# A decoder trunk in three-pass matmuls: the down projection as seven block products, interleaved with the next up projection

## Chip, cores, metric

The kernel runs on one core of a Trainium2 chip. The metric is the device time of one execution in microseconds (us); lower is better. In the profile PE is TensorE's matmuls and PEld its weight loads, DVE is VectorE, ACT is ScalarE, POOL is GpSimd, and SP is SyncE, which issues the loads of the weights.

## What is computed

Two pre-norm residual layers over 256 tokens with 2048 features. Each has a mixer (different kinds of attention, with one input and one output projection) and an MLP of hidden size 8192. The change touches the MLPs alone:

```python
D_MODEL = 2048; SEQ = 256; DEPTH = 2; D_FF = 4 * D_MODEL

def squared_relu_mlp(h, w_up, w_down):
    return jnp.square(jax.nn.relu(h @ w_up)) @ w_down

for layer in range(DEPTH):
    ...                                  # x = x + mixer(rms_norm(x))
    h = rms_norm(x, mlp_norm[layer])
    x = x + squared_relu_mlp(h, w_up[layer], w_down[layer])
return rms_norm(x, final_norm)
```

Everything is float32 in and out.

## The kernel before

**Three passes.** A float32 operand is split into a high half, rounded to the float32r format, and a low half, which is what is left. A product runs as wh·xh + wh·xl + wl·xh, summed in PSUM. Activations lie with features on the partitions, and an operand tile is `[xh | xl]`, 512 columns for 256 tokens. So for one K-tile (128 rows of K) and one column tile (128 columns of the weight) the kernel issues two matmuls with a piece of the weight as the stationary operand: one of 512 columns (wh against both halves, line 445) and one of 256 (wl against xh, line 446). That is the block kind "T". Some blocks of the mixers are of kind "N": there the activations are stationary and the weights move, in three matmuls of 256 columns (lines 434 to 436). The very last block of the program, kind "last", has weights stationary and three matmuls of 256 columns (lines 440 to 442).

**The weight stream.** All weights go through one list, `stream`, in the order in which TensorE uses them. An element is a chunk: 4 K-tiles x 256 columns, 16 matmuls. A `Unit` is one load from DRAM by SP (1 MB, 4 K-tiles x 512 columns, rows of 2 KB) and feeds two chunks. `hi_to` makes a chunk's high half with an ACT copy (line 1077), `lo_to` its low half with a DVE subtraction (line 1085), and `consume` issues the matmuls. There are 3 buffers for raw loads, 5 for high halves and 4 for low halves. The main loop for chunk i is, in this order:

```python
        hi_to(i + HI_BUFS)      # written up to the high half of chunk i + 4
        lo_to(i + LO_BUFS)      # written up to the low half of chunk i + 3
        chunk(i)                # the matmuls, and at a block's end its evacuation
        ...                     # jobs.tick(): side work (attention, norms, splits)
```

The order is fixed (a manual schedule), and each engine runs its own instructions in that order. The low half of chunk i + 3 lies in the buffer of chunk i - 1, the high half of chunk i + 4 in that of chunk i - 1 too.

**The MLP** (`mlp`). The hidden features are cut into two groups of 4096. For a group, the up projection runs in pairs of blocks of 256 columns, with 16 K-tiles each. `up_done` adds the two halves of PSUM, squares the positive part and splits the result into `h` (lines 935 to 937, 156, 157). Then the group's down projection runs as 8 blocks with 32 K-tiles each; `down_done` adds the result to the residual `xT` (lines 951 to 955). The low half of every chunk is made by DVE. POOL's queue issues hardly anything: a few constants, `odist`, `sk` and `fn`.

Of the kernel before, what the change touches and what calls it, by code (L numbers as in the profile page):

```python
# [38 lines left out]
class Jobs:  # L39
    """Side work (attention, norms, splits) that is woven between the weight chunks."""  # L40
# [48 lines left out]
class Ring:  # L89
    """Order of use of the buffers of one tag: a buffer is free once its key is done."""  # L90
# [13 lines left out]
class Unit:  # L104
    """One load: up to 4 K-tiles x 512 columns of a weight, for one or two chunks."""
# [5 lines left out]
class Chunk:  # L111
    """Some K-tiles of a block: views(raw) are the parts of the load in the order of the operand."""

    def __init__(self, unit, kts, views):
        self.unit, self.kts, self.views = unit, kts, views
        unit.users += 1


class Block:
    """256 output columns of one projection (128 where tiles is 1)."""  # L120

    def __init__(self, kind, chunks, mov, done, tiles=2):
        self.kind, self.chunks, self.mov, self.done, self.tiles = kind, chunks, mov, done, tiles
        self.total = sum(len(c.kts) for c in chunks)
        self.count, self.ps = 0, None
# [3 lines left out]
def trunk(ctx, tc, x, attn_norm, mlp_norm, w_up, w_down, ev_w_in, ev_q_norm, ev_w_uq, ev_kv_norm,  # L129
# [5 lines left out]
    psum = ctx.enter_context(tc.tile_pool(name="psum", bufs=1, space=bass.MemoryType.PSUM))  # L135
    ctx.enter_context(tc.manual_schedule())
# [48 lines left out]
    # the tensor engine's clock rises while the first loads are under way  # L185
    def keep_warm(n):
        if "warm" not in st:
            st["warm"] = psum.tile([P, 2, 512], F32, name="mm", bufs=3)[:, 0]
        ps = st["warm"]
        for _ in range(n):  # L190
            mm(ps, warm[:, 0:P], warm, start=True, stop=True)
# [19 lines left out]
    def make_xs(b, g0):  # L211
        """Next phase's moving operand from residual block b, and its sum of squares."""
# [19 lines left out]
    def sum_squares(acc, ms, size):  # L232
        """ms [P, 2] <- mean square + eps per token, tokens on partitions."""
# [5 lines left out]
    def broadcast(r, rB):  # L239
        """rB [P, T] <- r [P, 2] along the free axis, on every partition."""  # L240
# [46 lines left out]
    def w_chunks(w, c0, groups, width=512):  # L287
        """Loads of K-tile groups x width columns of w [K, N]: the chunks of each 256 columns."""
# [23 lines left out]
    def evac(ps, dst, scale=None, rB=None):  # L312
        """dst [P, 2, T] <- sum of the bank halves, times scale, times rB along tokens."""
# [11 lines left out]
    def scores(pairs, dist, cs, u):  # L325
        """u [P, 2, 384] <- biased logits of two heads: [q0 k0 | q1 k0 | q1 k1]."""
# [9 lines left out]
    def neg_max(u, nm):  # L336
        """nm [P, 2 (q tile), 2 (head)] <- -max."""
# [13 lines left out]
    def transpose_p(u):  # L351
        """In place: [k0 q0 | k0 q1 | k1 q1]."""
# [55 lines left out]
    stream = []  # L408

# [4 lines left out]
    def consume(block, i, hi, lo):  # L414
        if block.ps is None:
            block.ps = psum.tile([P, 2, 512], F32, name="mm", bufs=3)
            if block.kind == "last":
                block.ps = [block.ps[:, 0, 0:T], psum.tile([P, 2, 512], F32, name="mm", bufs=3)[:, 0, 0:T]]
# [9 lines left out]
        for n, j in order:  # L428
# [10 lines left out]
            if block.kind == "last":  # L439
# [14 lines left out]
    def even_mixer():  # L454
# [5 lines left out]
        def open_pool():  # L460
            pool = E["pool"] = pool_ctx.enter_context(tc.tile_pool(name="even", bufs=1, reuse_waits="tile"))
# [78 lines left out]
        # the shared rotary key, on both partition halves  # L540
# [11 lines left out]
        def rotate(src, n, outs):  # L552
            """outs <- src*cos + swap(src)*sin; src [P, n, T]."""
# [29 lines left out]
        # per-head projections  # L583
# [38 lines left out]
        def cut(view, pr, width, a, b):  # L622
            """The columns a:b of the two heads, width columns each, of a load."""
# [68 lines left out]
        # output projection  # L692
# [18 lines left out]
    def odd_mixer():  # L711
# [7 lines left out]
        def open_pool():  # L719
            pool = E["pool"] = pool_ctx.enter_context(tc.tile_pool(name="odd", bufs=1, reuse_waits="tile"))  # L720
# [78 lines left out]
        # dilated groups: slots 2*sp, 2*sp+1 of the three groups, one joint softmax  # L799
# [112 lines left out]
    def mlp(layer, last):  # L912
# [6 lines left out]
        def open_pool():  # L919
# [316 lines left out]
```

## Time and profile before

| what | value |
|---|---|
| time, three runs | 2188.19, 2188.74, 2188.99 us (median 2188.74) |
| span of the profiled execution | 2186.0 us; no time of that execution around its span is shown, and the median of the runs is 2.7 us longer |
| PE busy | 2173.6 us, 99% |
| DVE busy | 1298.6 us, 59% |
| ACT busy | 1022.6 us, 47% |
| POOL busy | 12.8 us |
| DMA | 396 MB, 181 GB/s over the span |

A matmul's duration in the profile is from its start to the modelled end of its pipeline, and overlaps the next one. So what a matmul costs is read from the distance of the starts. DVE and ACT instructions overlap a little too when they follow one another.

### The profile page before, as it was taken

The page shows a single profiled execution, that of the slowest core. Times are in us where ns is not written, and L with a number is a line of the kernel's source. Part 1 is how long each engine was busy: PE and PEld are TensorE (multiplying, and loading weights), DVE is VectorE, ACT ScalarE, POOL GpSimd, SP SyncE. Part 2 cuts the span into 40 slices and gives each one's busy share as a digit, 9 for nine tenths or more (in the row PEclk, how much of TensorE's full clock was granted, in tenths as well). Part 3 has the DMA queues.
Part 4 walks back from the last instruction along what each step waited for, and adds up shares of the span by engine and source line. Part 5 has one row for each costly group of instructions (what it writes and reads, how often), then busy time and mean ns, then how long its engine had stood idle before and what let it go on. Part 6 is the DMA issues. An engine that isn't in the chain of part 4 may idle for free.

```text
span 2186.0 us, 31244 instructions
## 1 busy us (share of the span) xinstructions
PE 2173.6 (99%) x12902; PEld 1917.1 (88%) x12902; DVE 1298.6 (59%) x1576; ACT 1022.6 (47%) x1377; POOL 12.8 (1%) x24
## 2 busy tenths in 40 slices
PE   9999999999999999999999999999999999999998
PEld 7898988888888888888888889988888888888887
DVE  6766666656545565556667665566565556655554
ACT  6554544444434444444445446444443334444443
POOL 0000000000000000000000000000000000000000
PEclk9999999999999999999999999999999999999999
DMA  8544455555555555655654456665555555555544
GB/s 260 182 149 155 147 188 184 184 194 175 198 187 192 191 182 187 207 190 176 188 166 148 154 174 190 158 193 184 186 183 199 185 184 189 192 185 183 191 154 135
DMA packets 211374, 396.26 MB, mean 181 GB/s; under 512 B 8904, under 2 KB 31504, under 8 KB 211104
## 3 DMA queue, kind: packets, MB, share of 16 engines
q1 hardware_dynamic: 210720, 392.33, 55.3%
q8 instruction: 101, 1.65, 0.3%
q0 software_dynamic: 480, 1.94, 0.3%
q14 instruction: 41, 0.34, 0.0%
q10 hardware_dynamic: 32, 0.01, 0.0%
HBM read 392.15 MB, written 2.10 MB: 180 GB/s over the span
## 4 chain that ended last, share of the span: by engine, by line
PE 99%; DMA 0%; ACT 0%; SPq 0%; DVE 0%; POOLq 0%; issue 0%; ACTq 0%; DVEq 0%
PE mm L445 55%; PE mm L446 30%; PE mm L448 3%; PE mm L435 2%; PE mm L434 2%; PE mm L436 2%; PE side L333 1%; PE side L356 1%; PE side L402 1%; PE side L331 1%; PE mm L442 0%; PE mm L440 0%; PE mm L441 0%; PE side L403 0%; DMA latqs<-ev_w_in 0%; PE side L873 0%
## 5 line engine op out<-in xcount | busy, mean ns | idle before, releaser
L1085 DVE TENSOR_TENSOR lo<-raw,hi 128x1024 fp32r<-128x1024 f32 (+1 forms) x756 | 898.6, 1194 | 627.2 <-PE mm L446 555.4
L1077 ACT ACTIVATE hi<-raw 128x1024 fp32r<-128x1024 f32 (+1 forms) x756 | 780.6, 1036 | 804.9 <-PE mm L445 712.4
L445 PE MATMUL mm<-xs,hi 128*128 128x512 f32 x2805 | 995.3, 396 | 0.5 <-ACT hi L1077 0.3
L446 PE MATMUL mm<-xs,lo 128*128 128x256 f32 x2992 | 820.5, 279 | 0.2 <-DVE lo L1085 0.2
L445 PE MATMUL mm<-h,hi 128*128 128x512 f32 x1922 | 675.0, 393 | 0.0
L445 PEld LDWEIGHTS mm<-xs,hi 128*128 128x128 f32 x2805 | 526.0, 188 | 121.1 <-ACT hi L1077 1.0
L446 PEld LDWEIGHTS mm<-xs,lo 128*128 128x128 f32 x2992 | 561.4, 188 | 8.8 <-DVE lo L1085 0.5
L446 PE MATMUL mm<-h,lo 128*128 128x256 f32 x1984 | 548.7, 279 | 0.0
L445 PEld LDWEIGHTS mm<-h,hi 128*128 128x128 f32 x1922 | 360.2, 187 | 84.4
L446 PEld LDWEIGHTS mm<-h,lo 128*128 128x128 f32 x1984 | 371.9, 187 | 2.8
L434 PE MATMUL mm<-hi,xs 128*128 128x256 f32 x320 | 91.8, 287 | 0.0
L936 DVE TENSOR_TENSOR t<-mm,t 128x512 f32<-128x512 f32 x64 | 44.3, 691 | 77.3 <-ACT t L935 77.3
L436 PE MATMUL mm<-hi,xs 128*128 128x256 f32 x320 | 89.7, 280 | 0.0
L435 PE MATMUL mm<-lo,xs 128*128 128x256 f32 x320 | 89.7, 280 | 0.0
L935 ACT ACTIVATE t<-mm 128x512 f32<-128x512 f32 x64 | 38.3, 598 | 100.3 <-PE mm L448 100.3
L448 PE MATMUL mm<-xs,hi 128*128 128x512 f32 x187 | 69.9, 396 | 0.0
L445 PE MATMUL mm<-oT,hi 128*128 128x512 f32 x192 | 67.6, 394 | 0.0
L435 PEld LDWEIGHTS mm<-lo,xs 128*128 128x128 f32 x320 | 60.3, 188 | 0.2
L434 PEld LDWEIGHTS mm<-hi,xs 128*128 128x128 f32 x320 | 60.3, 188 | 0.2
L436 PEld LDWEIGHTS mm<-hi,xs 128*128 128x128 f32 x320 | 60.2, 188 | 0.0
L446 PE MATMUL mm<-oT,lo 128*128 128x256 f32 x192 | 53.6, 279 | 0.0
L315 ACT ACTIVATE t<-mm 128x512 f32<-128x512 f32 x37 | 22.1, 598 | 53.8 <-PE mm L448 53.8
(266 smaller groups left out, 1494.3 us busy)
## 6 DMA issues: line engine op xcount, KB each, us to landing
raw<-w_up SPq DMA_DIRECT2D x128, 1024.0 KB, 5.3
raw<-w_down SPq DMA_DIRECT2D x120, 1024.0 KB, 5.0
raw<-od_w_in SPq DMA_DIRECT2D x36, 1024.0 KB, 5.1
raw<-ev_w_in SPq DMA_DIRECT2D x30, 1024.0 KB, 5.4
raw<-ev_w_out SPq DMA_DIRECT2D x16, 1024.0 KB, 5.0
raw<-od_w_in SPq DMA_DIRECT2D x20, 512.0 KB, 4.1
raw<-od_w_out SPq DMA_DIRECT2D x16, 512.0 KB, 6.0
raw<-w_down SPq DMA_DIRECT2D x16, 512.0 KB, 3.6
```

Of the source, the lines that this page charges most:

```text
L315: act(t, ps[:, :, T:], AF.Copy, scale=1.0 if scale is None else scale)
L331: mm(ps[:, 0:P], q[:, 0:P], k[:, 0:P], start=(i == 0), stop=(i == n - 1))
L434: mm(o, xh, hi[:, n], start=first, stop=False)
L435: mm(o, xh, lo[:, n], start=False, stop=False)
L436: mm(o, xl, hi[:, n], start=False, stop=last)
L445: mm(ps[:, j], hi[:, n, c], m, start=first, stop=False)
L446: mm(ps[:, j, 0:T], lo[:, n, c], m[:, 0:T], start=False, stop=False)
L448: mm(ps[:, j], hi[:, n, c], m, start=False, stop=True)
L935: act(t, ps[:, :, T:], AF.Copy)
L936: tt(t, ps[:, :, 0:T], t, op=OP.add)
L1077: act(d, r, AF.Copy)
L1085: tt(d, r, f32(h), op=OP.subtract)
```

## The change

The hidden features are cut into eight groups of 1024. In seven of the eight, the down projection is computed in block products: for two K-tiles, two halves of the tokens and two halves of 512 output columns, the eight products of a 2 x 2 block multiplication become seven, of sums and differences of the blocks. Each is again three matmuls of 256 columns, with the activation as the stationary operand. The last group stays plain (kind "T", one block at a time).

- `up_done` makes the sums of the activation blocks (`S1` to `S4`) with four small DVE operations and splits all seven with one ACT and one DVE operation.
- A product unit is still a load of 4 K-tiles x 512 columns; it feeds four chunks: `plain` (two blocks, 12 matmuls), `single` (one block, 6 matmuls), `13` and `24` (12 each). The weight sums of the last two are made by DVE in `prep13` and `prep24` before the split.
- The seven products of a 512-column stretch gather in four PSUM banks over a group (`s0`: three of them, `s1`: four). ACT copies them to SBUF, and a DMA on POOL's queue writes them to a DRAM tile (`sums`), adding to it from the second group on. After the seventh group `combine` reads a tile back, forms the four results, scales them with the token norms, turns them with TensorE and adds them to `xT`.
- Up blocks become kind "U": three matmuls of 256 columns in place of a pair, all into 256 columns of PSUM; their load is 8 K-tiles x 256 columns (rows of 1 KB) and feeds two chunks.
- The stream of a group's products is interleaved with the next group's up projection: two product chunks, one up chunk, and so on. The first group's up projection and the last group's down projection stand alone.
- For every second up chunk from the second group on (`again`), the low half isn't made by DVE: ACT writes the negated, rounded weights into the low half's buffer, and a DMA on POOL's queue adds the weights from DRAM to it.
- Comments are taken out, and the PSUM banks are opened by phase.

```diff
-        NGRP = 2
+        NGRP = 8
         W = FF // NGRP
...
+    X11, X22, X12, S1, S2, S3, S4 = range(7)
+    HOME = {1: ("s0", 0), 2: ("s0", 1), 3: ("s0", 2), 5: ("s1", 0), 7: ("s1", 1), 6: ("s1", 2), 4: ("s1", 3)}
...
+            if block.kind == "U":
+                mm(ps[:, j], hi[:, n, c], m[:, 0:T], start=first and j == 0, stop=False)
+                mm(ps[:, j], hi[:, n, c], m[:, T:], start=False, stop=False)
+                mm(ps[:, j], lo[:, n, c], m[:, 0:T], start=False, stop=last and j == 1)
...
+    def consume_products(block, i, hi, lo):
...
+        for o, (a, prod) in enumerate(chunk.prods):
+            half, at = HOME[prod]
+            if half not in block.ps:
+                block.ps[half] = banks(half, 1)
+            ps = block.ps[half].rearrange("p b c -> p (b c)")[:, at * T:(at + 1) * T]
+            for q, pr in enumerate(chunk.kts):
+                x = block.mov(pr)
...
+                mm(ps, x[:, a, 0:P], hi[:, o, q], start=first and at % 2 == 0, stop=False)
+                mm(ps, x[:, a, 0:P], lo[:, o, q], start=False, stop=False)
+                mm(ps, x[:, a, P:], hi[:, o, q], start=False, stop=last and (at % 2 == 1 or prod == 3))
+        block.count += 1
+        if block.count == block.total - 2:
+            block.done("s0", block.ps["s0"])
+        if block.count == block.total:
+            block.done("s1", block.ps["s1"])
...
         def up_done(grp, b):
             def f(ps):
-                r = E["pool"].tile([P, 2, T], F32, name="hr", bufs=3)
                 t = temp()
-                act(t, ps[:, :, T:], AF.Copy)
-                tt(t, ps[:, :, 0:T], t, op=OP.add)
-                stt(r, t, 0.0, t, op0=OP.max, op1=OP.mult)
+                act(t, ps, AF.Relu)
+                r = E["pool"].tile([P, 8, P], F32, name="hr", bufs=1)
+                act(r[:, 0:4].rearrange("p (j k) t -> p j (k t)", j=2), t, AF.Square)
...
+                        tt(r[:, 4], r[:, 0], r[:, 2], op=OP.add)
+                        tt(r[:, 6], r[:, 1], r[:, 0], op=OP.subtract)
+                        tt(r[:, 5], r[:, 4], r[:, 1], op=OP.subtract)
+                        tt(r[:, 7], r[:, 3], r[:, 5], op=OP.subtract)
+                        act(h[:, :, 0:P], r[:, 1:8], AF.Copy)
+                        tt(h[:, :, P:], r[:, 1:8], f32(h[:, :, 0:P]), op=OP.subtract)
...
+                def prep13(unit=unit, made=made):
+                    w = blocks(unit.raw)
+                    t = made[13] = E["pool"].tile([P, 1024], F32, name="w13")
+                    tt(four(t), w[:, :, :, 1].rearrange("p q k c -> p k q c"),
+                       w[:, :, 0].rearrange("p q h c -> p h q c"), op=OP.subtract)
+
+                def prep24(unit=unit, made=made):
+                    w = blocks(unit.raw)
+                    t = made[24] = E["pool"].tile([P, 1024], F32, name="w24")
+                    tt(four(t)[:, 0], four(made[13])[:, 1], w[:, :, 0, 0], op=OP.add)
+                    tt(four(t)[:, 1], w[:, :, 1, 0], four(t)[:, 0], op=OP.subtract)
...
+                chunks += [Chunk(unit, ks, plain, prods=((X11, 1), (X12, 2))),
+                           Chunk(unit, ks, single, prods=((S4, 3),)),
+                           Chunk(unit, ks, of(13), prep13, ((S1, 5), (S3, 7))),
+                           Chunk(unit, ks, of(24), prep24, ((S2, 6), (X22, 4)))]
...
+        def products_done(grp, cb):
+            def f(half, ps):
+                n = 3 if half == "s0" else 4
+                stage = E["pool"].tile([P, 4 * T], F32, name="stage", bufs=2)[:, 0:n * T]
+                act(stage, ps.rearrange("p b c -> p (b c)")[:, 0:n * T], AF.Copy)
+                to = sums[cb][:, 0:n * T] if half == "s0" else sums[cb][:, 3 * T:]
+                if grp == 0:
+                    nc.gpsimd.dma_start(to, stage)
+                else:
+                    nc.gpsimd.dma_start(to, stage, accum_op=OP.add)
+                if grp == NGRP - 2 and half == "s1":
+                    jobs.spawn(combine(cb), keys=[("sum", cb)], delay=1)
...
+        def combine(cb):
+
+            s = E["pool"].tile([P, 7, 2 * P], F32, name="hs", bufs=2 * nb)
+            nc.gpsimd.dma_start(s, sums[cb].rearrange("p (o c) -> p o c", o=7))
+            yield 3, 0
...
+        stream.extend(up_list(0))
+        for grp in range(NGRP - 1):
+            s, u = product_list(grp), up_list(grp + 1)
+            for i in range(len(u)):
+                stream.extend(s[2 * i:2 * i + 2] + u[i:i + 1])
...
+            prep = stream[i][0].chunks[stream[i][1]].prep
+            if prep:
+                prep()
             for d, r in views(i, his[i]):
                 act(d, r, AF.Copy)
...
+            again = stream[i][0].chunks[stream[i][1]].again
             for (d, r), (h, _) in zip(views(i, los[i]), views(i, his[i])):
-                tt(d, r, f32(h), op=OP.subtract)
+                if again is None:
+                    tt(d, r, f32(h), op=OP.subtract)
+                else:
+                    act(d, r, AF.Copy, scale=-1.0)
+                    nc.gpsimd.dma_start(d.rearrange("p (k c) -> p k c", c=T), again, accum_op=OP.add)
```

## Rows read from the trace of the kernel before

**Rows 1.** The page: span, busy times by engine, and the chain by engine.
```profile
span 2186.0 us, 31244 instructions
...
PE 2173.6 (99%) x12902; PEld 1917.1 (88%) x12902; DVE 1298.6 (59%) x1576; ACT 1022.6 (47%) x1377; POOL 12.8 (1%) x24
...
PE 99%; DMA 0%; ACT 0%; SPq 0%; DVE 0%; POOLq 0%; issue 0%; ACTq 0%; DVEq 0%
```
**Rows 2.** Timeline of PE, first MLP: start, duration, engine, line, operation, tiles, count.
```profile
798.76 0.39 PE L445 MATMUL mm<-xs,hi 128*128 128x512 f32 x1
799.00 0.28 PE L446 MATMUL mm<-xs,lo 128*128 128x256 f32 x1
799.11 0.39 PE L445 MATMUL mm<-xs,hi 128*128 128x512 f32 x1
```
**Rows 3.** Timeline of PE, kind "N", second mixer: first and last of 100 starts.
```profile
1364.76 0.28 PE L436 MATMUL mm<-hi,xs 128*128 128x256 f32 x1
...
1376.37 0.28 PE L436 MATMUL mm<-hi,xs 128*128 128x256 f32 x1
```
**Rows 4.** Timeline of PE, kind "last": first and last of 28 starts.
```profile
2168.33 0.28 PE L441 MATMUL mm<-h,hi 128*128 128x256 f32 x1
...
2171.57 0.28 PE L441 MATMUL mm<-h,hi 128*128 128x256 f32 x1
```
**Rows 5.** Timeline of DVE, then of ACT, first MLP; in brackets idle time before.
```profile
639.28 1.23 DVE L1085 TENSOR_TENSOR lo<-raw,hi 128x1024 fp32r<-128x1024 f32 x1 [1.56 <-PE mm L446]
642.08 1.23 DVE L1085 TENSOR_TENSOR lo<-raw,hi 128x1024 fp32r<-128x1024 f32 x1 [1.57 <-PE mm L446]
...
639.16 1.06 ACT L1077 ACTIVATE hi<-raw 128x1024 fp32r<-128x1024 f32 x1 [1.79 <-PE mm L445]
641.96 1.06 ACT L1077 ACTIVATE hi<-raw 128x1024 fp32r<-128x1024 f32 x1 [1.74 <-PE mm L445]
```
**Rows 6.** Groups by line and form: busy us, mean ns; idle before, its releasers.
```profile
L1085 DVE TENSOR_TENSOR lo<-raw,hi 128x1024 fp32r<-128x1024 f32 x716 | 872.8, 1222 | 614.1 <-PE mm L446 551.0 <-PE mm L435 36.2 <-issue 18.8
L1077 ACT ACTIVATE hi<-raw 128x1024 fp32r<-128x1024 f32 x716 | 757.4, 1059 | 788.0 <-PE mm L445 700.4 <-issue 25.2 <-DMA raw<-w_down 17.5
...
L1085 DVE TENSOR_TENSOR lo<-raw,hi 128x512 fp32r<-128x512 f32 x40 | 25.8, 686 | 13.1 <-issue 7.1 <-PE mm L446 4.4 <-PE mm L435 1.6
L1077 ACT ACTIVATE hi<-raw 128x512 fp32r<-128x512 f32 x40 | 23.2, 624 | 16.9 <-PE mm L445 12.1 <-issue 3.1 <-DMA raw<-od_w_in 0.9
```
**Rows 7.** The chain in order of time: start, us, four transposes at the program's start.
```profile
16.04 0.44 PE side L1110 x4
```
**Rows 8.** Timeline of DVE and of ACT where nothing is waited for.
```profile
1079.07 1.22 DVE L1085 TENSOR_TENSOR lo<-raw,hi 128x1024 fp32r<-128x1024 f32 x1
1080.21 0.68 DVE L952 TENSOR_TENSOR t<-mm,t 128x512 f32<-128x512 f32 x1
...
2127.53 1.05 ACT L1077 ACTIVATE hi<-raw 128x1024 fp32r<-128x1024 f32 x1
2128.48 0.62 ACT L227 ACTIVATE t<-xT 128x512 f32<-128x512 f32 x1
```
**Rows 9.** DMA issues over the span: count, KB each, median us to landing.
```profile
raw<-od_w_in SPq DMA_DIRECT2D x20, 512.0 KB, 4.1
...
raw<-w_down SPq DMA_DIRECT2D x16, 512.0 KB, 3.6
...
fn<-final_norm POOLq DMA_DIRECT2D x1, 1024.0 KB, 5.7
odist<-c_dist POOLq DMA_DIRECT2D x1, 768.0 KB, 6.8
...
sk<-od_sinks POOLq DMA_DIRECT2D x1, 8.0 KB, 2.8
```
**Rows 10.** DMA in 1080 to 1110, 2130 to 2160, 1500 to 1600 us.
```profile
q1 hardware_dynamic: 6336, 6.29, 67.3%
...
raw<-od_w_in SPq DMA_DIRECT2D x14, 512.0 KB, 4.5
...
q1 hardware_dynamic: 5647, 5.60, 59.2%
...
raw<-w_down SPq DMA_DIRECT2D x10, 512.0 KB, 4.5
...
q1 hardware_dynamic: 9503, 18.88, 57.9%
```

More of the change, by code (lines that the diff above doesn't have):

```diff
@@ L111, with __init__ @@
 class Chunk:
-    def __init__(self, unit, kts, views):
-        self.unit, self.kts, self.views = unit, kts, views
+    def __init__(self, unit, kts, views, prep=None, prods=(), again=None):
+        self.unit, self.kts, self.views, self.prep, self.prods = unit, kts, views, prep, prods
+        self.again = again
         unit.users += 1
 class Block:
-    def __init__(self, kind, chunks, mov, done, tiles=2):
+    def __init__(self, kind, chunks, mov, done, tiles=2, take=None):
         self.kind, self.chunks, self.mov, self.done, self.tiles = kind, chunks, mov, done, tiles
-        self.total = sum(len(c.kts) for c in chunks)
+        self.total = len(chunks) if kind == "S" else sum(len(c.kts) for c in chunks)
+        self.take = take
         self.count, self.ps = 0, None
@@ L414, in consume @@
     def consume(block, i, hi, lo):
+        if block.kind == "S":
+            return consume_products(block, i, hi, lo)
         if block.ps is None:
-            block.ps = psum.tile([P, 2, 512], F32, name="mm", bufs=3)
-            if block.kind == "last":
-                block.ps = [block.ps[:, 0, 0:T], psum.tile([P, 2, 512], F32, name="mm", bufs=3)[:, 0, 0:T]]
+            block.ps = (block.take or banks)()
         ps, tiles, kts = block.ps, block.tiles, block.chunks[i].kts
@@ L451, in consume @@
             block.done(ps)
+    def consume_products(block, i, hi, lo):
+        chunk = block.chunks[i]
+        if block.ps is None:
+            block.ps = {}
+        n = len(chunk.prods)
+        hi = hi[:, 0:n * 2 * T].rearrange("p (o q c) -> p o q c", q=2, c=T)
+        lo = lo[:, 0:n * 2 * T].rearrange("p (o q c) -> p o q c", q=2, c=T)
+        for o, (a, prod) in enumerate(chunk.prods):
[5 more added lines that the diff above has]
+                x = block.mov(pr)
+                first, last = block.count < 4 and q == 0, block.count >= block.total - 4 and q == 1
+                mm(ps, x[:, a, 0:P], hi[:, o, q], start=first and at % 2 == 0, stop=False)
[6 more added lines that the diff above has]
+            block.done("s1", block.ps["s1"])
     def even_mixer():
@@ L948, in f, with finish, down_done @@
+        left = [2] * 8
+        def finish(b):
+            left[b] -= 1
+            if left[b] == 0:
+                if last:
+                    final_block(E, b)
+                else:
+                    x_done(b, g_next, 2)
+        def down_done(b):
             def f(ps):
@@ new lines, in f, with eights, load, views @@
+                finish(b)
+            return f
+        def eights(w, c0, n, by_dma=False):
+            view = w.rearrange("(k p) c -> p k c", p=P)
+            chunks = []
+            for a in range(0, n, 8):
+                def load(raw, a=a):
+                    nc.sync.dma_start(raw.rearrange("p (k c) -> p k c", c=T), view[:, a:a + 8, c0:c0 + T])
+                unit = Unit(load)
+                for h in range(2):
+                    def views(raw, dst, h=h):
+                        return [(dst, raw[:, h * 1024:(h + 1) * 1024])]
+                    k = a + 4 * h
+                    chunks.append(Chunk(unit, list(range(k, k + 4)), views,
+                                        again=view[:, k:k + 4, c0:c0 + T] if h and by_dma else None))
+            return chunks
@@ new lines, in up_list, with product_list, mov @@
+        def up_list(grp):
+            blocks = [Block("U", eights(up, grp * W + b * T, KT, grp > 0), mov, up_done(grp, b), take=take_up)
+                      for b in range(nb)]
+            return [(block, i) for block in blocks for i in range(len(block.chunks))]
+        def product_list(grp):
+            def mov(pr):
+                need(("h", layer, grp, pr))
+                return hs[grp, pr]
+            blocks = [Block("S", product_chunks(down[grp * W:(grp + 1) * W], cb * 512), mov, products_done(grp, cb))
+                      for cb in range(4)]
+            return [(block, i) for block in blocks for i in range(len(block.chunks))]
@@ new lines, in mlp, with h_mov @@
+        stream.extend(up_list(0))
[3 more added lines that the diff above has]
+                stream.extend(s[2 * i:2 * i + 2] + u[i:i + 1])
+        def h_mov(kt):
+            need(("h", layer, NGRP - 1, kt // 2))
+            return hs[NGRP - 1, kt // 2][:, kt % 2]
+        wd = down[FF - W:]
+        for b in range(8):
+            if last and b == 7:
+                add(Block("last", eights(wd, b * T, W // P), h_mov, lambda ps: last_block(E, ps), take=take_last))
+            else:
+                add(Block("T", eights(wd, b * T, W // P), h_mov, down_done(b), take=take_down(b)))
@@ L1189, in trunk @@
         block, c = stream[i]
-        if block.tiles * len(block.chunks[c].kts) == 8:
+        if block.tiles * len(block.chunks[c].kts) == 8 or block.kind == "S" and c % 2:
             jobs.tick()
```

102 lines of the change are left out of this document (73 added, 29 removed).

## The prediction

> **What bounds the kernel now.** I read the page's busy times and chain first: TensorE is busy for 99% of the 2186.0 us and carries 99% of the chain that ended last [rows 1]. So only two things can change the time: the matmul work itself, and a new wait in front of a matmul. Next I read the spacing of matmul starts, because the modelled durations overlap: a 512-column matmul and the 256-column one behind it take 0.350 us together (798.76 to 799.11) [rows 2]. Where three 256-column matmuls stand in place of such a pair, 99 starts take 11.61 us, 0.1173 us each, with activations as the stationary operand [rows 3]; with weights stationary and the tokens moving, as in the very last block, 27 starts take 3.24 us, 0.120 us each [rows 4]. None of them waits for its weight load. Last I read how far the splitters run ahead: in the MLP, ACT makes a high half and DVE a low half every 2.80 us, the time of one chunk on TensorE, and each starts when TensorE gives a buffer back [rows 5]; over the span that is what ended most of their idle time [rows 6]. So a low half is started when its buffer comes free, four chunks ahead, and no earlier. It has three chunks of TensorE time to be finished in. Today that is 8.4 us for a 1.2 us operation.
>
> **The change on TensorE.** Seven of eight groups of a down projection become products. A group was 8 K-tiles x 16 column tiles = 128 pairs, 128 x 0.350 = 44.8 us. It becomes 16 block products of 7 x 3 matmuls, 336 x 0.1173 = 39.4 us (the stationary operand is an activation, as in rows 3). Over 14 groups: -75.4 us. The up projections' 2 x 1024 pairs become three 256-column matmuls; weights are stationary, so rows 4 is nearest: 0.360 for 0.350, +20.5 us (by rows 3 it would be +3.9). Putting the sums back turns 64 blocks of 128x128; four of them take 0.44 us [rows 7], +7.0 us. The first up group and the last, plain down group have no partner and cost what they cost today. Together 2186.0 - 75.4 + 20.5 + 7.0 = 2138.1 us for the profiled span, or 2121.5 with the cheap up chunks. The median of the runs is 2.7 us above that span, so **2141** (2124) if nothing waits.
>
> **The change on DVE and ACT.** The stream repeats a period of six chunks: two product chunks (12 and 6 matmuls), an up chunk (24), two product chunks (12, 12), an up chunk (24). On TensorE: 42 x 0.1173 + 48 x 0.120 = 10.69 us; there are 8 per group, 14 groups, 112 periods. Back to back a 1024-column operation costs DVE 1.14 us and ACT 0.95 us from start to start [rows 8]; 512 columns cost up to 0.69 and 0.62 [rows 6]. DVE per period: low halves of three product chunks and one up chunk 4 x 1.14, of the short chunk 0.69, prep13 1.14, prep24 2 x 0.69, and half of the four small adds and the split in `up_done` (about 2 us, an estimate from the same rows), 1.0: 8.8 us, 82%. Without the DMAs it would be 9.9. ACT: six high halves 5 x 0.95 + 0.62, one negated copy 0.95, half of two stagings (0.7 and 0.95) and of `up_done`'s work (about 2): 8.1 us, 76%. Both fit, and their in-order queues have three chunks of cover; I cost them at nothing. If DVE missed it, a period would grow by what it lacks, and no more.
>
> **The wait that is added.** Every second up chunk no longer gets its low half from DVE. ACT writes minus the rounded weights, and a DMA on POOL's queue adds the weights from DRAM. It has the same place in the stream: its buffer comes free when the short product chunk ends, and it is needed after one up chunk and two product chunks: 2.88 + 1.41 + 1.41 = 5.70 us. In that time ACT first makes the next high half, whose buffer came free at the same moment and which is written ahead of it (0.95), then the negated copy (1.06), and in every second period the staging of the first three products stands before both (0.7, three quarters of 0.95): 2.36 us on average. What is left for the DMA from issue to landing is 3.34 us. TensorE goes through the chunks in order, so what is missing is idle time, and the loop starts again only when the chunk is done: it is paid 112 times. Queued behind the waiting DMA on POOL are the next group's stagings and, late, the read-back of the sums, none of them near their use.
>
> No such accumulating DMA is in this trace, so I bound its landing by rows. Below: 2.8 us, an 8 KB load from POOL; then it is hidden. 512 KB weight loads land in 3.6 to 4.1 us as a median over the span [rows 9], and in 4.5 us in the two stretches of 512 KB loads, at 59 and 67% of the DMA engines [rows 10]. Above: 5.7 us for 1 MB and 6.8 us for 768 KB from POOL [rows 9]. If an accumulation reads both its operands, it moves as much as 1 MB does. When it is issued the engines are not idle: the up unit's load is released at the end of the chunk before, and the next product unit's by the same negated copy. I take **4.7 us**, nearest to the 4.5 of the same bytes beside a busy stream. Then 4.7 - 3.34 = 1.36 us per period, x 112 = 152 us. By the ends: 0 and (6.8 - 3.34) x 112 = 388 us.
>
> The Trainium skill, "Collectives: The Full Stack", section "The bandwidth ceiling: the fold count and why AG ≠ RS ≠ AR", speaks against the change: an add inside a DMA reads two sources, and a transfer with it ran at 1/1.93 of the rate of a plain one. No run here shows such an add yet. By an estimate from that factor, 512 KB would land like 1 MB of [rows 9], and the sum would be 2402 instead of 2290 us.
>
> **Other costs.** The stagings write 128x768 and 128x1024 to DRAM, from POOL, accumulating from the second group on; their PSUM halves are next used some 8 us later, and ACT empties them in under 1 us, so nothing. The read-back waits for the last staging to land (about 5 us) and itself for about 5 us, while its adds come three ticks (about 8 us) later in DVE's order: up to 2 or 3 us of DVE waiting, eight times, 0 to 24 us; the low halves' lead covers that, I take 0 and keep 24 for the range. Up loads change from rows of 2 KB to 1 KB, which cost no more: 5.6 MB in 30 us at a 59.2% share and 18.88 MB in 100 us at 57.9% [rows 10] are 315 and 326 GB/s of a full share.
>
> **Rivals.**
> *A, the forecast:* TensorE waits for DMA-made low halves, 2138 + 152 = 2290, as a median **2293**.
> *B, hidden:* the DMA lands within 3.3 us and the arithmetic wins: **2141**, 2124 with cheap up chunks. For it: 2.8 us for a small POOL load, 3.6 us for 512 KB. The point at which it decides is a landing of 3.34 + (2189 - 2141)/112 = 3.77 us; below, the kernel is faster than before. Against it: every 512 KB row of a stretch of its own is above 4.
> The Trainium skill, "DMA: Bandwidth & Descriptors", section "Anatomy of one DMA — SWDGE (gpsimd) path", gives 2.0 us plus the bytes over 436 GB/s; by that estimate 512 KB take 3.2 us, nothing is missing, and the sum is B's. The traces speak rather against: 1 MB from POOL took 5.7 us beside the stream, where the fit gives 4.4.
> *C, the DMA engines become the bound:* a period moves two loads of 1.05 MB, 0.52 MB added to low halves and 0.46 MB of staging; counted twice where it accumulates, 4.06 MB. At 326 GB/s that is 12.5 us against 10.69, x 112 = +198 us, **2339**. Counted once it is 3.08 MB, 9.4 us, and no bound. The waits would then end on `raw` loads as well, not on low halves alone.
> *D, the products are not there, or the splitters bind:* if DVE ran at its full durations (1.22 for 1.14) it would need about 9.3 us of 10.69, still no bound; that gives B's time.
>
> **How the numbers follow.** A 0.50, B with D 0.33 (of it 0.03 with a landing so near 3.77 us that nothing is seen), C 0.17 (of it 0.02 near no change). A measurement of this kernel tells about 0.2% from no change. So faster 0.30, same 0.05, slower 0.65. The range takes in B's 2141 and a little of its cheap end, and A with a landing of about 6.3 us, (6.3 - 3.34) x 112 = 332 us, with some of the read-backs: 2130 to 2480. A's own range is 2190 to 2480.
>
> **What will show it.** In the changed profile TensorE's share falls to about 93%, with idle time in front of the up chunks' matmuls that read `lo`, ended by DMA `lo<-w_up`; these DMAs are 112 and land in 4 to 6 us. A product chunk of 12 matmuls takes 1.41 us and an up chunk 2.88 us. DVE stands near 80% inside the product stretch. If the DMAs land in 3.3 us and TensorE stays at 99%, B is right and my landing time wrong; if it waits for `hi` or `raw`, C is; if DVE has no idle time left, D's sum was wrong.

## The result and the profile after

The changed kernel takes 3362.7 us (median of 4 runs, 3353.4 to 3366.6) against 2188.5 us: 1.536 times the time before, 95% interval 1.534 to 1.538. It is slower, as forecast, but by 1174 us where 104 were forecast, and far outside the range of 2130 to 2480. In the experiments below a time that stands without an interval is that of a single run.

Lines of the page of the changed kernel: span and busy times, the granted clock (PEclk) and the DMA queues. They answer to [rows 1]; the second fence has the clock and the load queue of the kernel before.

```profile
span 3351.6 us, 39749 instructions
...
PE 2383.0 (71%) x16086; PEld 2275.5 (68%) x16086; DVE 1631.1 (49%) x2136; ACT 1431.5 (43%) x1889; POOL 256.5 (8%) x256
...
PE   9999956665565566665899999666655566666667
...
PEclk9999987777787777777999999777777778778778
...
q1 hardware_dynamic: 280224, 392.32, 36.9%
q0 software_dynamic: 76384, 119.39, 20.6%
```
```profile
PEclk9999999999999999999999999999999999999999
...
q1 hardware_dynamic: 210720, 392.33, 55.3%
```

TensorE is busy for 71% of the span where it was 99%, and its idle slices are the two product stretches. In the same slices the granted clock is 0.7 to 0.8; before it was full nearly throughout. DVE and ACT have more work than before (1631 and 1432 us busy), but over the longer span DVE's share fell to 49% and ACT's to 43%, and the load queue's fell from 55% to 37%; POOL's queue rose from 0.3% to 20.6%. No engine is near its limit. This is a wait, not a shortage of an engine.

The waits of the changed kernel (who waited for whom, us in total, times, longest) name it, and the DMA issues (count, KB, median us to landing; last, for the low halves, minimum, median and maximum) show what came so late; they answer to [rows 9].

```profile
PE up L467 <- DMA lo<-w_up: 945.8, 112, 11.2
...
raw<-w_up SPq DMA_DIRECT2D x128, 1024.0 KB, 7.1
raw<-w_down SPq DMA_DIRECT2D x128, 1024.0 KB, 5.9
lo<-w_up POOLq DMA_DIRECT2D x112, 512.0 KB, 9.0
...
DMA to landing us min/median/max: 7.6/9.0/12.8
```

There are 112 waits, one per period, 8.4 us each in the mean, all in front of the first matmul that reads a DMA-made low half. The accumulating DMA lands after 9.0 us in the median, 7.6 at the least and 12.8 at the most.

The timeline of two periods shows the whole loop. The first fence is PE at the two waits and around the first, the second ACT and POOL before them, the third the loads that SP starts just before POOL's DMAs.

```profile
899.16 0.28 PE L465 MATMUL up<-xs,hi 128*128 128x256 f32 x1
...
902.04 0.28 PE L498 MATMUL s<-hi,hs 128*128 128x256 f32 x1
...
904.89 0.28 PE L465 MATMUL up<-xs,hi 128*128 128x256 f32 x1
...
915.27 0.55 PE L467 MATMUL up<-xs,lo 128*128 128x256 f32 x1 [9.98 <-DMA lo<-w_up]
915.62 0.42 PE L465 MATMUL up<-xs,hi 128*128 128x256 f32 x1
915.83 0.42 PE L466 MATMUL up<-xs,hi 128*128 128x256 f32 x1
...
922.08 0.29 PE L465 MATMUL up<-xs,hi 128*128 128x256 f32 x1
...
936.37 0.55 PE L467 MATMUL up<-xs,lo 128*128 128x256 f32 x1 [8.18 <-DMA lo<-w_up]
```
```profile
899.68 0.79 ACT L1074 ACTIVATE stage<-s 128x768 f32<-128x768 f32 x1
900.37 1.05 ACT L1280 ACTIVATE hi<-raw 128x1024 fp32r<-128x1024 f32 x1
901.31 1.04 ACT L1292 ACTIVATE lo<-raw 128x1024 fp32r<-128x1024 f32 x1
...
902.65 1.30 POOL L1293 DMA_DIRECT2D lo<-w_up  x1 [1.00 <-ACT lo L1292]
...
924.66 0.95 ACT L1017 ACTIVATE hs<-hr 128x896 fp32r<-128x896 f32 x1 [1.33 <-DVE hr L1016]
925.52 1.04 ACT L1280 ACTIVATE hi<-raw 128x1024 fp32r<-128x1024 f32 x1
926.47 1.05 ACT L1292 ACTIVATE lo<-raw 128x1024 fp32r<-128x1024 f32 x1
...
927.81 1.30 POOL L1293 DMA_DIRECT2D lo<-w_up  x1 [19.94 <-ACT lo L1292]
```
```profile
902.38 0.37 SPq L1031 DMA_DIRECT2D raw<-w_down  x1
...
927.54 0.37 SPq L1031 DMA_DIRECT2D raw<-w_down  x1
```

At 899.16 the up chunk starts whose predecessor gave the buffer back. It takes 2.88 us, the two product chunks 2.85 us, and at 904.89 the waiting chunk starts: 5.73 us of lead, as worked out. But POOL issues the DMA at 902.65, 3.5 us after the buffer came free, because ACT does the staging, the next high half and the negated copy first; and it lands 12.6 us later. In the next period the buffer comes free at 922.08 and the issue is at 927.81, 5.7 us later: ACT's order there holds the splitting of the activations, which itself waits 1.33 us for DVE. That DMA lands in 8.6 us. In both periods the same negated copy lets SP start a load of 1 MB, 0.27 us ahead of POOL's DMA. The two periods alternate over the whole trace: half of the 112 DMAs have a staging DMA in flight when they are issued and land in 11.2 us in the mean, the others in 8.6. Over all 112 the mean way to the issue is 4.5 us and the mean landing 9.9; with 5.7 us of lead that leaves 8.7 us, of which the chunk's first two matmuls hide 0.2.

After each wait the matmul starts are 0.21 us apart (915.62 to 915.83) in place of 0.12: the lower of the two clock levels, 1.2 GHz.

### The profile page after: what moved, and what is told of

Its sections match the earlier page's. It is cut to its first block, busy times and chain, and to the rows that moved or that the text cites. A ratio compares the mean times of both kernels' runs of the same rounds, so it can differ in the third digit from the quotient of the medians.

```text
span 3351.6 us, 39749 instructions
## 1 busy us (share of the span) xinstructions
PE 2383.0 (71%) x16086; PEld 2275.5 (68%) x16086; DVE 1631.1 (49%) x2136; ACT 1431.5 (43%) x1889; POOL 256.5 (8%) x256
## 3 DMA queue, kind: packets, MB, share of 16 engines
q0 software_dynamic: 76384, 119.39, 20.6%
## 5 line engine op out<-in xcount | busy, mean ns | idle before, releaser
L467 PE MATMUL up<-xs,lo 128*128 128x256 f32 x2048 | 694.5, 339 | 945.8 <-DMA lo<-w_up 945.8
L467 PEld LDWEIGHTS up<-xs,lo 128*128 128x128 f32 x2048 | 493.2, 241 | 965.0 <-issue 965.0
L465 PE MATMUL up<-xs,hi 128*128 128x256 f32 x2048 | 670.3, 327 | 1.6 <-DVE xT L759 1.6
L466 PE MATMUL up<-xs,hi 128*128 128x256 f32 x2048 | 667.8, 326 | 0.0
L465 PEld LDWEIGHTS up<-xs,hi 128*128 128x128 f32 x2048 | 487.8, 238 | 1.9 <-ACT hi L1280 1.9
L466 PEld LDWEIGHTS up<-xs,hi 128*128 128x128 f32 x2048 | 483.5, 236 | 0.0
L498 PE MATMUL s<-hi,hs 128*128 128x256 f32 x1568 | 450.3, 287 | 0.0
L499 PE MATMUL s<-lo,hs 128*128 128x256 f32 x1568 | 447.8, 286 | 0.0
L500 PE MATMUL s<-hi,hs 128*128 128x256 f32 x1568 | 445.3, 284 | 0.0
L474 PE MATMUL mm<-xs,hi 128*128 128x512 f32 x885 | 320.7, 402 | 0.0
L498 PEld LDWEIGHTS s<-hi,hs 128*128 128x128 f32 x1568 | 308.3, 197 | 0.0
L500 PEld LDWEIGHTS s<-hi,hs 128*128 128x128 f32 x1568 | 303.4, 194 | 0.0
L475 PE MATMUL mm<-xs,lo 128*128 128x256 f32 x944 | 260.1, 281 | 0.2 <-DVE lo L1290 0.2
L475 PEld LDWEIGHTS mm<-xs,lo 128*128 128x128 f32 x944 | 178.4, 189 | 3.1 <-DVE lo L1290 0.5
## 6 DMA issues: line engine op xcount, KB each, us to landing
sums<-stage POOLq DMA_DIRECT2D x56, 512.0 KB, 10.8
```

The lines of the kernel that those rows point to most:

```text
L465: mm(ps[:, j], hi[:, n, c], m[:, 0:T], start=first and j == 0, stop=False)
L466: mm(ps[:, j], hi[:, n, c], m[:, T:], start=False, stop=False)
L467: mm(ps[:, j], lo[:, n, c], m[:, 0:T], start=False, stop=last and j == 1)
L474: mm(ps[:, j], hi[:, n, c], m, start=first, stop=False)
L475: mm(ps[:, j, 0:T], lo[:, n, c], m[:, 0:T], start=False, stop=False)
L498: mm(ps, x[:, a, 0:P], hi[:, o, q], start=first and at % 2 == 0, stop=False)
```

## The experiments

**Theory 1** after the result: the loss is TensorE's wait for the DMA-made low halves, and the clock that falls in it. **Rival 2:** the staging DMAs, or the DMA engines as a whole, hold everything up. **Rival 3:** the products overload DVE, and the DMAs only hide that.

### Without the DMAs

```diff
-            blocks = [Block("U", eights(up, grp * W + b * T, KT, grp > 0), mov, up_done(grp, b), take=take_up)
+            blocks = [Block("U", eights(up, grp * W + b * T, KT), mov, up_done(grp, b), take=take_up)
```

> All low halves of the up projection are made by DVE again; everything else of the change stays (seven products, staging, the sums in DRAM). Theory 1 (the whole loss is TensorE's wait for the 112 low halves that a DMA makes, 946 us in the changed profile, and the slower clock after each wait): 2138 us by the sum of the prediction, plus 1.5 ns for each of 4704 product matmuls, so about 2150 us, TensorE at 97% or more and the granted clock at 1.0. Rival 2 (the staging DMAs, or the DMA engines as a whole, are what delays): still above 2600. Rival 3 (DVE cannot make them all, 9.9 of 10.7 us per period): 2200 to 2350, with TensorE waiting for DVE's lo.

Measured: 2226.7 us, 1.0173 times before (1.0160 to 1.0187). One argument takes back 1136 of the 1174 us. The staging is still there, so rival 2 falls; in the product stretches (500 to 900 us) TensorE is 98% busy and waits for DVE's low halves for 12.7 us over the whole span, so rival 3 falls as well: with all low halves to make, DVE is 90% busy there and late by little. The DMA engines are busier in this run than in the changed kernel (83% of the time against 58%), and TensorE waits for none of these transfers. But 2227 is 77 us above the 2150 of the expectation, and still slower than before. The waits of this kernel show a cause (the last line has the busy times of PE, PEld, DVE, ACT and POOL, the clock, the DMA share and GB/s from 500 to 900 us):

```profile
ACT hr L1100 <- DVE hr L1097: 47.2, 8, 8.0
...
PE side L1107 <- ACT hr L1100: 42.5, 11, 8.6
...
DVE t L1092 <- DMA hs<-sums: 38.2, 8, 8.4
...
PE up L467 <- DVE lo L1290: 12.7, 29, 0.9
...
500.00:900.00 400.00, 393.38 (x3268) 390.04 (x3267) 358.09 (x417) 264.88 (x309) 31.14 (x36) 1.00 0.83 232
```

It is the read-back of the sums in `combine`: DVE's adds wait for the DMA, ACT's scaling for the adds, and the transposes stand in TensorE's order before the scaled result is there.

### A plain DMA in place of the accumulating one

```diff
-                    nc.gpsimd.dma_start(d.rearrange("p (k c) -> p k c", c=T), again, accum_op=OP.add)
+                    nc.gpsimd.dma_start(d.rearrange("p (k c) -> p k c", c=T), again)
```

> The DMA that adds the weights to the negated high half becomes one that only writes them; this leaves out the addition, so the low half is a plain copy of the weights. If the accumulation is what makes the landing long (a 1 KB packet takes 102 ns with it, against 46 ns for a load's), the landing falls from 9.0 to about 7 us (32 packets per engine x 56 ns = 1.8 us), and the time by 1.8 x 112 = 200 us and something for the clock, to about 3100 us. If the start from POOL's queue is the larger part, it stays within 100 us of 3360. Were the accumulation all of it, the landing would be near the 4.5 us of such loads and the time near 2300 us.

Measured: 3104 us. The same 512 KB land in 6.5 us in place of 9.0, and TensorE waits 690.7 us in place of 945.8. The accumulation is a part of the landing, 2.5 us, and not the larger one: the plain DMA in this place misses the 3.3 us of lead as well. In the packets of the trace, the median for 1 KB is 102 ns with the addition and 61 without, and 46 for a load of SP's.

```profile
PE up L467 <- DMA lo<-w_up: 690.7, 111, 9.2
...
lo<-w_up POOLq DMA_DIRECT2D x112, 512.0 KB, 6.5
```

### Half as many bytes

```diff
-                    act(d, r, AF.Copy, scale=-1.0)
-                    nc.gpsimd.dma_start(d.rearrange("p (k c) -> p k c", c=T), again, accum_op=OP.add)
+                    act(d[:, 0:512], r[:, 0:512], AF.Copy, scale=-1.0)
+                    nc.gpsimd.dma_start(d[:, 0:512].rearrange("p (k c) -> p k c", c=T), again[:, 0:2], accum_op=OP.add)
+                    tt(d[:, 512:], r[:, 512:], f32(h[:, 512:]), op=OP.subtract)
```

> The same 112 accumulating DMAs carry half as much: two of the four K-tiles (256 KB), and DVE makes the low half of the other two. If the bytes and the engines they share set the landing, it halves from 9.0 to about 4.5 us, the wait nearly goes (4.5 - 3.3 = 1.2 us a period, 130 us) and the time is about 2400 us. If the start from POOL's queue sets it (a landing with some 5 us that do not depend on the size), it is 6.5 to 7.5 us, the wait about 600 us, and the time 2900 to 3050 us.

Measured: 3024.9 us, a landing of 6.9 us, a wait of 608.4 us.

```profile
PE up L467 <- DMA lo<-w_up: 608.4, 112, 7.2
...
lo<-w_up POOLq DMA_DIRECT2D x112, 256.0 KB, 6.9
```

Half the bytes take 2.1 us off. A line through these two sizes has 4.8 us that don't depend on the size and 4.2 us for 512 KB. By that line, which two points can't test, the part without bytes is alone longer than the 3.34 us that the prediction had left, and no size of such a DMA would have been hidden in this place. The 4.8 us hold for this place alone: a 1 MB load starts at about the same moment, and no edit separates what it takes from the DMA.

### Without the staging writes

```diff
                 if grp == 0:
                     nc.gpsimd.dma_start(to, stage)
-                else:
-                    nc.gpsimd.dma_start(to, stage, accum_op=OP.add)
```

> The stagings of the second to seventh group are not written to DRAM; this leaves their sums out. ACT still empties PSUM. Theory 1: the low halves' DMAs have POOL's queue for themselves, all land in the 7.6 us of the fastest ones, and a period loses 1.5 to 2.5 us: 3100 to 3200 us. Rival 2 (the staging DMAs hold up the low halves): 2600 or less. No effect: 3360.

Measured: 3225.9 us, a landing of 8.7 us (8.0 to 12.0), a wait of 818.5 us; the time is 26 us above the upper end expected.

```profile
PE up L467 <- DMA lo<-w_up: 818.5, 112, 9.5
...
lo<-w_up POOLq DMA_DIRECT2D x112, 512.0 KB, 8.7
```

The staging costs the low halves some 1.1 us per period, less than expected. What goes is the longer landing of every second period: 11.2 us in the mean becomes 8.8, and the 8.6 of the others stays. With POOL's queue to themselves, but still behind SP's load, they are no faster than 8 us. Rival 2 is a small part.

### TensorE kept busy through the wait

```diff
+FILL = 36
...
         block, c = stream[i]
+        if block.chunks[c].again is not None:
+            ps = side()
+            for _ in range(FILL):
+                mm(ps, xs_all[:, 0, 0:P], xs_all[:, 0], start=True, stop=True)
         consume(block, c, his.pop(i), los.pop(i))
```

> 36 matmuls of 512 columns whose result nobody reads stand ahead of each up chunk with a DMA-made low half, 36 x 0.233 = 8.4 us in place of the mean wait of 8.4 us. No work of the change is taken away. If the clock after each wait costs what the matmul durations of the changed profile suggest (2383 us of busy time against 2138, so some 245 us), the granted clock stays at 1.0 and the time falls to 3050 to 3200 us although TensorE has 940 us more work. If the clock costs nothing, the time stays at 3360 or grows.

Measured: 3153.8 us, 209 us less with 36 x 112 matmuls more, and a mean granted clock of 0.996 against 0.841. TensorE waits for the DMAs for 55.8 us only; the added matmuls fill the rest. The busy times (first line; the kernel with the later read-back, below, has the second, for the 16086 matmuls of the changed kernel) give the size of the fill:

```profile
PE 3074.0 (98%) x20118; PEld 2811.0 (89%) x20118; DVE 1631.1 (52%) x2136; ACT 1432.6 (45%) x1889; POOL 256.6 (8%) x256
...
PE up L468 <- DMA lo<-w_up: 55.8, 64, 3.0
```
```profile
PE 2142.2 (98%) x16086; PEld 2044.7 (94%) x16086; DVE 1743.0 (80%) x2248; ACT 1314.0 (60%) x1777; POOL 109.1 (5%) x144
```

The 4032 added matmuls take 3074.0 - 2142.2 = 932 us. With the 56 us of wait that is 42 us more than the 946 us that they replace, and the profiled execution is still 200 us shorter: the clock after the waits costs about 240 us of the 1174, and the waits themselves the 946. A second reading agrees: the same 16086 matmuls are busy for 2383.0 us in the changed kernel, 241 us more than where TensorE hardly waits.

### More lead, in the first MLP

```diff
             for d, r in views(i, his[i]):
                 act(d, r, AF.Copy)
             at["hi"] += 1
+            j = i + 3
+            if j < phases[2][0] and stream[j][0].chunks[stream[j][1]].again is not None:
+                chunk_j = stream[j][0].chunks[stream[j][1]]
+                early_lo[j] = LOD[0].tile([P, 1024], F32R, name="lod", bufs=2)
+                for d, r in chunk_j.views(chunk_j.unit.raw, early_lo[j]):
+                    act(d, r, AF.Copy, scale=-1.0)
+                    nc.gpsimd.dma_start(d.rearrange("p (k c) -> p k c", c=T), chunk_j.again, accum_op=OP.add)
...
-            los[i] = wts.tile([P, 1024], F32R, name="lo", bufs=LO_BUFS)
+            los[i] = early_lo[i] if i in early_lo else wts.tile([P, 1024], F32R, name="lo", bufs=LO_BUFS)
...
-                if again is None:
+                if i not in early_lo:
                     tt(d, r, f32(h), op=OP.subtract)
-                else:
-                    act(d, r, AF.Copy, scale=-1.0)
-                    nc.gpsimd.dma_start(d.rearrange("p (k c) -> p k c", c=T), again, accum_op=OP.add)
```

> In the first MLP alone, the DMA-made low halves get two buffers of their own and are started four chunks earlier, with the high half of the unit's first chunk; in the second MLP they stay as in the changed kernel. Nothing is left out. If the wait comes from three chunks of lead (5.7 us) against a landing of 9 to 12.8 us, the lead is now about 12 us in the first MLP: its wait falls from 473 to under 100 us and its clock stays near 1.0, so about 2750 to 2850 us in all. If the DMA engines or POOL's queue cannot deliver a low half per period at all, the first MLP stays within 100 us of the second.

Measured: 2378 us. The expectation misdescribes its kernel: as the diff shows, the second MLP has no DMA-made low halves at all here; DVE makes them. So the total can't be held against 2750 to 2850, and the first MLP alone is to be read, against the first MLP of the run without DMAs. There the wait for the DMAs is 18.5 us, where the changed kernel's 56 waits of 8.4 us come to 473: lead is what was missing. The landing itself is shorter here: the same accumulating 512 KB land in 6.5 us, the fastest in 6.0, with the next load of SP started 1.4 us behind them and not 0.27 us ahead. So the 9.0 us are not what such a DMA takes everywhere. What makes it longer in the changed kernel's place is not shown: this run changes the place and the lead together, and no run the place alone. The first MLP is not as fast as without the DMAs: from its first to its last up matmul it takes 835 us against 688, which is nearly all of the 151 us that the total lies above that run. The waits of PE from 400 to 1200 us and the busy times (PE, PEld, DVE, ACT, POOL, clock, DMA share, GB/s) show what is late next:

```profile
PE up L466 <- ACT hi L1281: 40.8, 28, 2.7
PE side L1108 <- ACT hr L1101: 30.2, 3, 11.3
PE up L468 <- DVE lo L1297: 23.9, 34, 0.8
PE up L468 <- DMA lod<-w_up: 18.5, 15, 3.3
...
lod<-w_up POOLq DMA_DIRECT2D x56, 512.0 KB, 6.5
...
DMA to landing us min/median/max: 6.0/6.5/9.8
...
500.00:900.00 400.00, 345.01 (x2591) 332.24 (x2590) 252.77 (x301) 235.34 (x274) 62.65 (x58) 0.94 0.88 224
```

The DMA engines are 88% busy, and over the span ACT waits 315.9 us for loads of `w_up` (longest 7.1). In the run without the DMAs the engines were 83% busy and ACT waited 171.9 us (longest 4.4), but SP's loads landed in 6.1 and 6.8 us in the first MLP, where they take 10.6 and 10.8 now (450 to 1000 us there, to 1150 us here). With the lead mended, rival C of the prediction seems to begin: the transfers are in each other's way. That is read from the trace; no edit tests it. As built here, the accumulating DMAs lose even when they are early.

### The read-back later

Two kernels without the DMAs. A tick is one turn of the main loop. The first has both edits below; the second leaves the adds at 3 ticks and has the transposes 3 ticks after them, where the changed kernel has 1 and the first has 2.

```diff
-            yield 3, 0
+            yield 6, 0
             p1, p2, p3, p5, p7, p6, p4 = (s[:, i] for i in range(7))
...
                 act(g[:, tok], g[:, tok], AF.Copy, scale=r[:, tok:tok + 1])
-            yield 1, 1
+            yield 2, 1
```

> The kernel without the DMA-made low halves, and besides the read-back of the sums has 6 ticks instead of 3 before its adds, and its transposes come 2 ticks instead of 1 after them. If what is left of the 2227 us over the sum of 2150 is the wait for the read-back (TensorE stood 42.5 us before its transposes of hr, DVE 38.2 us for hs<-sums, and the clock fell after each), the time falls by 45 to 65 us, to 2162 to 2182, under the kernel before. If the loss lies in the product stretches, it stays above 2215.

> As the other, but only the transposes are later (3 ticks after the adds instead of 1); the adds keep their 3 ticks. If TensorE's wait is for the scaled result alone, this takes most of it: 2180 to 2195. If DVE's wait for the read-back holds up the low halves as well, it stays some 15 to 30 us above the run with both.

Measured: 2182.9 us with both, 0.9973 times before (0.9962 to 0.9983), 1 us above the upper end expected: **faster than the kernel before**, by 0.27%, without the part of the change that made the loss. With the later transposes alone 2220.8 us, 1.0149 times (1.0134 to 1.0165): a miss, 26 us above the upper end expected. TensorE's wait at the transposes was the last link only; while DVE stands before the read-back, the low halves behind it in DVE's order stand too, and TensorE waits for them (first fence, 38.9 us in place of 12.7). With both edits the waits of PE that are left are small, and TensorE is 99% busy in the product stretches (second fence):

```profile
PE up L467 <- DVE lo L1290: 38.9, 24, 7.6
```
```profile
PE up L467 <- DVE lo L1290: 8.6, 21, 1.1
...
500.00:900.00 400.00, 396.46 (x3301) 393.88 (x3301) 362.35 (x420) 268.10 (x311) 31.23 (x36) 1.00 0.84 235
```

### The up projections as pairs again

On top of both edits, up blocks are of kind "T" with one two-bank PSUM tile and the evacuation that adds the two halves:

```diff
-            return st["banks"].tile([P, 2, T], F32, name="up", bufs=2)
+            return banks("up", 1)
...
-                act(t, ps, AF.Relu)
+                act(t, ps[:, :, T:], AF.Copy)
+                tt(t, ps[:, :, 0:T], t, op=OP.add)
+                act(t, t, AF.Relu)
...
-            blocks = [Block("U", eights(up, grp * W + b * T, KT), mov, up_done(grp, b), take=take_up)
+            blocks = [Block("T", eights(up, grp * W + b * T, KT), mov, up_done(grp, b), take=take_up if grp else take_down(b))
```

> The kernel without DMA-made low halves and with the later read-back (2183 us), and the up projections run again as pairs of a 512-column and a 256-column matmul into two PSUM banks, with the evacuation that belongs to them. The prediction's sum charged 0.360 against 0.350 us for each of 2048 pairs. If that term is right and the evacuation hides behind the product chunks that follow, the time falls by 12 to 22 us, to 2161 to 2171. If the single up bank or the added DVE work (0.7 us per up block on an engine 90% busy) makes TensorE wait, it stays at 2183 or grows, with waits on t or on lo.

Measured: 2255.0 us, 1.0299 times before (1.0285 to 1.0313), so 72 us lost in place of 12 to 22 won. Now DVE is late: TensorE waits for its low halves. For the single up bank, the other suspect of the expectation, it waits little (last line).

```profile
PE up L475 <- DVE lo L1292: 79.1, 54, 1.8
...
PE up L474 <- DVE t L1003: 4.4, 6, 1.4
```

DVE is 88% busy in the product stretches of this kernel, where it was 91% in the faster one, but of a longer period: by the matmuls counted (74 a period here, 90 there) it is 10.2 us per period in place of 9.9. What is added is 0.7 us per up block, with a wait for ACT inside it (80.8 us over the span), and by this trace that is enough to use up the lead. So "U" pays for its 10 ns a pair with a cheaper evacuation, which the prediction did not count as a gain.

## Why the prediction was wrong, point by point

- **What bounds the kernel, and where a wait would enter:** right. One low half in six chunks came late, 112 times, in the place named, and its lead was 5.73 us where 5.70 were worked out.
- **The landing of the accumulating DMA, 4.7 us:** the step that failed. It measured 9.0 us in the median, 9.9 in the mean, and 12.6 and 8.6 in the two periods shown; that is 5.2 of the 7.3 us by which a period came out longer than the sum (8.7 where 1.36 stood). The rows that I took it from were SP's loads and plain loads from POOL, and I chose the one of the same bytes. The run with half the bytes shows 4.8 us independent of size in this place, the plain DMA 2.5 us for the addition, the run without staging about 1.1 us a period for its neighbours on POOL's queue, the stagings, which I had costed at nothing. Started in another place, in the run with more lead, the same DMA took 6.5 us: I had named the load that the same negated copy releases, and took it as covered by a row from beside a busy stream (4.5 us). How much of the 9 us it takes stays open. Even the upper end, 6.8 us of 768 KB, was too low.
- **The way to the issue, 2.36 us:** also too small. It took 3.5 and 5.7 us in the two periods shown and 4.5 in the mean, the other 2.2 of the 7.3 us, since ACT's order holds the activations' split too. No run tests ACT's order by itself. I had costed ACT at nothing because its sum was 76% of a period; but the negated copy stands in that order, and its lead has no slack to give. By the prediction's own formula these two periods lose 3.5 + 12.6 - 5.7 = 10.4 us and 5.7 + 8.6 - 5.7 = 8.6 us; the trace has 9.98 and 8.18 (the chunk's first two matmuls need no low half).
- **The clock:** left out of the sum and of the range. TensorE had been idle for 6 to 11 us each time, and came back at the lower level; that is about 240 us, as the filled run and the busy times show. The Trainium skill, "TensorE: Matmul & The Clock Gate", section "The HAM clock gate (the "warmup" mystery)", says that TensorE's clock falls to half when it has been idle; the trace agrees (0.21 us between starts after a wait, 0.12 before), and with my 1.4 us of idle a period I had not looked for it.
- **The TensorE sum, 2138 us with no wait:** too low by 39 us against the 2176.9 us of the profile of the kernel with the later read-back, the fastest of its seven executions. There 3301 matmuls take 396.46 us, 0.1201 us each, where the sum mixes 0.1173 and 0.120 to 0.1187: over 10080 matmuls 14 us. The idle 3.5 us in 400 are some 10 us over the 1200 us of product stretches. Over the span TensorE is idle for 34.7 us where it was 12.4 in the kernel before, so another 12 us are idle time outside these stretches; about 3 us are left. The 0.120 for "U" was right (0.36 for three, 2.88 for a chunk).
- **The read-back, 0, at most 24 us:** wrong, though the changed kernel hardly shows it. Without the DMAs the read-back cost about 44 us (2226.7 to 2182.9): the cover that I named, the low halves' lead, was too short for it, and does not hold for TensorE's own transposes behind it. In the changed kernel itself TensorE waited only 3.8 us at the transposes.
- **The rivals:** B (hidden) was far off, with a decision point of 3.77 us against a landing of 9. The fit of the Trainium skill's "DMA: Bandwidth & Descriptors", section "Anatomy of one DMA — SWDGE (gpsimd) path", that stood beside it gives 3.2 us for 512 KB. The plain DMA of the weights took 6.5 us behind SP's load, but in the run without the DMAs the first group's plain stagings of 512 KB, which go to DRAM, landed in 3.0 us at the fastest: the fit is met there, and was not where this kernel needed it. The Trainium skill's "Collectives: The Full Stack", section "The bandwidth ceiling: the fold count and why AG ≠ RS ≠ AR", puts a plain transfer at 1.93 times the rate of one with an add; here the packets took 102 ns for 61, a ratio of 1.67. C was not the bound here (the load queue's share fell), and may be next once the lead is there. D was right in that DVE does not bind, even at 90% in the run without the DMAs, and the pairs show how near it is.

Together: 2176.9 us for the kernel whose TensorE hardly waits, 945.8 us of waits and 241 us of clock make 3364, against a span of 3351.6 us. The 12 us too many are mostly small waits of the first kernel that the changed one does not have. That the kernel came out slower, as forecast, owes to the mechanism, which was right; the size was wrong, in the landing above all.

## What to carry to other kernels

Where buffers are handed round, work out the lead of a step, from the moment its buffer comes free to its first reader, and hold it against the whole way of the new path: what stands ahead of it in each engine's order, the issue, and a landing measured for that kind of DMA. An engine with idle time is not yet slack: a slow path that is needed once per period costs its lateness every period, however idle everything else is, and here the idle TensorE paid again by its clock. And give the consumers of a DMA round trip through DRAM a later place in every in-order queue, not only in the last one.

## What the runs showed of the hardware

An accumulating DMA of 512 KB from POOL's queue landed in 8.6 us in the mean when a 1 MB load had been started 0.27 us ahead of it, in 11.2 with a staging DMA in flight as well, and in 6.5 (median) in the run where the next load came 1.4 us behind it; what of this the loads cause, no run separates. In the changed kernel's place, two sizes give some 4.8 us that do not depend on the size. The issue itself takes 1.29 us on POOL with the addition and 0.76 without. And 932 us of useless matmuls in the gaps made the kernel 209 us faster, by the clock alone.
